# Weights asked for earlier, token columns made later, and two blocks' residual steps sharing the attention: one change to a two-layer fp32 trunk

## The chip, the cores and the metric

The kernel runs on one core of a Trainium2 chip. The metric is the device time of one execution in microseconds (us). The kernel before was timed three times: 2561.57, 2564.88 and 2570.34 us, median 2564.88 us. TensorE is called PE, VectorE DVE, ScalarE ACT, GpSimd POOL, and the queue that issues the DMAs SP.

## The reference

1056 tokens (1024 prompt frames and 32 frames of a running stream) of width 1024 go through two layers in fp32. Each sub-layer normalises its input, and normalises its output before adding it to the residual:

```python
def rms_norm(x, w):
    return x * rsqrt(mean(x * x) + NORM_EPS) * w
# layer 0: gated linear recurrence (HGRN2); layer 1: window attention
x = x + rms_norm(mix, norm_mix_post[layer])
hf = rms_norm(x, norm_ffn_pre[layer])
a, b = split(hf @ w_ffn_in[layer], 2)
x = x + rms_norm((silu(a) * b) @ w_ffn_out[layer], norm_ffn_post[layer])
```

Between the layers, K and V for layer 1 come from one projection of the normalised residual: `k, v = split(rms_norm(x, kv_norm) @ w_kv, 2)`, with a rotation by position on K and on the queries. In layer 1, 16 query heads in 4 groups attend over a window of 128 earlier frames and their own chunk, with a learned sink per head.

## The kernel before

Features lie on the 128 partitions (8 groups, `KT`), tokens along the free axis in three blocks b = 0, 1, 2 of 384, 384 and 288 columns. An fp32 product is three matmuls of split operands: high by high, high by low, low by high. A weight unit is 128x1024 numbers (512 KB): one DMA into `wst` (two buffers), a cast to `wh` on ACT (L102, or L98 where the weight is scaled on the way) and the difference `wl` on DVE (L103, or L99 in four pieces). `wh` and `wl` have four buffers each. `wpair` makes the two units of one column group. The products of a dense stage are L133 (weights stand still, features come out on partitions), L145 (tokens come out on partitions) and L501 (the FFN's output). The accumulators in PSUM (`mm`) have four buffers.

The stages run in this order: the mixer of layer 0; its output projection `outproj` (L133, weights `wao`); the FFN (its input products L133 and L410, its output L501 into `mix`); K, V and Q projections (`kproj`, `vproj1`, `qproj`); the window attention; its `outproj` (weights `wbo`); the second FFN.

The residual's steps are the generator `postnorm`. It sums squares over partitions with a matmul by ones (L180 in `rnorm`, fed by squares on ACT and their running sum `acc` on POOL, L174), takes the inverse root on DVE and ACT (L155 to L163, result `rb`), and then for each of 8 feature groups multiplies (L243) and adds the old residual `xo` (L244), which a DMA brings from DRAM. It splits the result into `xh` (ACT) and `xl` (L210 on DVE), squares it, and sums again for the next norm (a second L180). With `tok=True` a tiny matmul against the identity (L193 in `rcol`) then turns the row `rb` into a token column `rt`; `vproj1` scales V by it.

The caller takes such steps between its own products with `go(generator, n)` and `step(b)`. A scheduler orders each engine's instructions by where they stand in the program and by when they could run; on the chip each engine takes its own list strictly in order, so an instruction that must wait holds all that stand behind it on its engine.

In the FFN's output, block b's products at feature k stand beside the residual's steps of block b-1 by the table `steps`. In the attention, a unit u (0 to 12) is one query group and one 128-token tile: scores `sc` (L1231), a maximum on DVE, exponentials on ACT, a product with the inverse sum (`P`, L1258), transposes `ptp` on PE (L1271), copies `pts`, and the product with V, `pav` (L1289). `plan[b][u]` says which other generators take a step there: `OP[b]` is block b's `outproj` with its residual. `OP[0]` and `OP[1]` use one buffer `mixb` for the projection's output, so that `OP[1]` can't write its output before `OP[0]`'s residual is read.

Of the kernel before, what the change touches and what calls it, by code (L numbers as in the profile page):

```python
# [59 lines left out]
def build(nc, tc, I, O):  # L60
# [45 lines left out]
    def wpair(arr, i, scale=None):  # L106
        return [wunit(arr[2 * i + k], None if scale is None else (scale, 4 * k)) for k in range(2)]
# [107 lines left out]
    def postnorm(b, mix, acc, w2, xold, wnext, spill, yout, done, more=None, full=None, tok=False):  # L215
# [38 lines left out]
        if yout is None:  # L254
# [3 lines left out]
            r = None  # L258
# [19 lines left out]
            done(xs, r, rb)  # L278


    def ffn(L, nx, post1, post, wmix, v1, w2, xold, wnext, spill, yout, res):
# [12 lines left out]
        def fin_half(j, b, half):  # L294
            if j not in wu:
                wu[j] = wpair(I[f"wfi{L}"], j)
# [67 lines left out]
        fin_ev(1, 2, pc, fin_half(1, 2, 1))  # L364
        t123(0)
# [147 lines left out]
        def step(b):  # L513
            if b not in ts:
                c0, W = BL[b]

                def done(*r):
# [4 lines left out]
                                 lambda: mp.tile([128, 384], F32, tag="xo", name="xo", bufs=3), tok=True)  # L522
# [26 lines left out]
        steps = {1: (1, 1, 1, 1, 1, 1, 1, 1), 2: (1, 1, 1, 1, 1, 1, 0, 1)}  # L549
        for b in range(NB):  # L550
            gload(3, b)
        for b in range(NB):
# [4 lines left out]
            def first(k):  # L557
                if k % 2 == 0:
                    un[0] = wfo(2, k // 2)
# [5 lines left out]
            for k in range(KT):  # L565
                if k not in pss:
                    first(k)
                fmul(pss[k], 3, b, wfo(3, k), 0, False, True)
# [51 lines left out]
    mbt = [None] * NB  # L620
    os = [None] * NB
    nx = [None] * NB

    def outproj(b, arr, pre, w2, xold, wnext, spill):
# [3 lines left out]
        mix = mbt[b] = mbs[b].tile([128, KT, 384], F32, tag="mixb", name="mixb", bufs=1)  # L628
# [24 lines left out]
    with tc.tile_pool(name="hp", bufs=1) as hp, \  # L653
# [45 lines left out]
        def vproj(p, b):  # L699
            units = wpair(I["wi"], p)  # L700
            W = BL[b][1]
            vt = vts[p, b] = hp.tile([128, 3, 256], F32, tag="vt", name="vt", bufs=2)
            for jl in range(3):
                rows = min(128, W - jl * 128)
                ps = mmps()
                mm_tm(ps, rows, units, xs[b][0], xs[b][1], jl * 128)
                yield
                nc.scalar.activation(vt[:rows, jl, :], ps[:rows, :256], AF.Copy, scale=rts[b][:rows, jl:jl + 1])  # L708

        v0 = vproj(0, 0)  # L710

        def gproj(p, b):
            units = wpair(I["wg"], p)
# [20 lines left out]
        def stage_a(c, h, b):  # L734
            W = BL[b][1]
            Wp = 384 if W == 384 else 320
            units = first_units if h == b == 0 else wpair(I["wfq"], h)
# [13 lines left out]
            if h == b == 0:  # L751
                go(xl0)
                go(v0)
                go(xl0)
                go(v0)
# [241 lines left out]
        def op0(b):  # L997
            return outproj(b, I["wao"], "a_out", "mix_post0", xin, "ffn_pre0", xs0d)
# [72 lines left out]
    late_pool = [ap, ap, None]  # L1071
# [31 lines left out]

    def kproj(b, units):
# [8 lines left out]
        kb = kbs[b] = late_pool[b].tile([128, 4, 128 + W], F32, name=f"kb{b}")  # L1113
        for du in range(2):
            rs = slice(du * 64, du * 64 + 64)
            if b > 0:
                nc.sync.dma_start(kb[rs, :, 0:128], kds[b - 1].rearrange("g hf r t -> (hf r) g t")[:, :, 256:384])
            nc.sync.dma_start(kb[rs, :, 128:128 + W], kd.rearrange("g hf r t -> (hf r) g t"))
        if b == 2:
# [3 lines left out]
    def vproj1(b, units):  # L1123
# [32 lines left out]
    uk = wpair(I["wk"], 0, scale="kv")  # L1156
# [10 lines left out]
    run(gk)  # L1167
    go(f0)
    uv = wpair(I["wv"], 0, scale="kv")
# [10 lines left out]
    late_pool[2] = ap2  # L1180
    os = [None] * NB
    nx = [None] * NB
    with tc.tile_pool(name="aps", bufs=1, space=PSUM, reuse_waits="tile") as aps:
# [17 lines left out]
        def qload():  # L1201
            b, g = order.pop(0)
            W = BL[b][1]
            qt = ap2.tile([128, 2, W], F32, tag="qt", name="qt", bufs=4)
# [262 lines left out]
```

## Time and profile before

| | |
|---|---|
| median of three runs | 2564.88 us (2561.57 to 2570.34) |
| the profiled execution | 2563.79 us |
| its span, first to last instruction | 2562.0 us |
| mean granted TensorE clock | 0.984 of full |
| PE busy | 2475.2 us, 97% |
| DVE busy | 1714.7 us, 67% |
| ACT busy | 1102.5 us, 43% |
| POOL busy | 451.9 us, 18% |

Times in the views count from the first instruction. A busy PE is not a PE at its full pace: matmuls overlap, and at the lower of its two clocks a matmul that keeps PE busy takes longer. So a stretch is read by three numbers together: busy time, number of matmuls, and granted clock. In a line of waits, "<-" names what the engine waited for.

### The profile page before, as it was taken

The numbers are of one execution on the slowest core, as the hardware profiler recorded it, in microseconds if no ns is written. First come the engines' busy times: TensorE is split into PE (matmuls) and PEld (weight loads), VectorE is DVE, ScalarE is ACT, GpSimd is POOL, SyncE is SP. The second block draws the span as 40 slices with busy tenths as digits, with TensorE's granted clock in tenths as the row PEclk, the third lists the DMA queues.
The fourth block names the chain that finished last, engine by engine and source line by source line (L and its number), as shares of the span: only waits on it lengthen the run. The fifth ranks groups of instructions, "written<-read, shape, count | busy, mean of one in ns | idle before, by whom it ended". The sixth has DMA issues, their size and how long they took to land.

```text
span 2562.0 us, 44049 instructions
## 1 busy us (share of the span) xinstructions
PE 2475.2 (97%) x17124; PEld 2375.9 (93%) x17124; DVE 1714.7 (67%) x3510; ACT 1102.5 (43%) x2395; POOL 451.9 (18%) x644
## 2 busy tenths in 40 slices
PE   7999998999999999999998999989999999999997
PEld 6999998998999999999997997758899999999997
DVE  8888789887776666642467647777876666652456
ACT  6555556665533333341344324556533333342332
POOL 5543444331200000000133311111300000000021
PEclk9999999999999999999999999989999999999998
DMA  5233333443422222251455542223422222252454
GB/s 176 85 104 99 123 121 121 133 133 105 144 77 82 82 79 75 75 174 63 158 164 159 175 132 78 66 71 103 153 87 77 75 75 76 77 176 76 150 174 145
DMA packets 124153, 287.98 MB, mean 112 GB/s; under 512 B 13432, under 2 KB 68632, under 8 KB 123944
## 3 DMA queue, kind: packets, MB, share of 16 engines
q1 hardware_dynamic: 123944, 285.17, 34.9%
q8 instruction: 134, 2.20, 0.3%
q14 instruction: 75, 0.61, 0.1%
HBM read 237.25 MB, written 48.07 MB: 111 GB/s over the span
## 4 chain that ended last, share of the span: by engine, by line
PE 73%; DVE 13%; DMA 5%; ACT 4%; issue 3%; POOL 1%; SPq 0%; POOLq 0%; DVEq 0%; ACTq 0%
PE mm L133 25%; PE mm L501 16%; PE mm L410 14%; PE c L410 6%; PE mm L145 5%; DVE wl L103 2%; PE sc L1231 1%; ACT wh L102 1%; PE pav L1289 1%; PE ptp L1271 1%; DMA xl<-g 1%; DMA wst<-in_wfq 1%; DVE mixb L244 1%; DMA wst<-in_wfo 1%; DVE xl L210 1%
## 5 line engine op out<-in xcount | busy, mean ns | idle before, releaser
L133 PE MATMUL mm<-xh,wh 128*128 128x384 f32 (+1 forms) x1968 | 633.1, 322 | 10.5 <-ACT xh L212 7.5
L133 PE MATMUL mm<-xh,wl 128*128 128x384 f32 (+1 forms) x1968 | 624.7, 317 | 5.3 <-DVE wl L99 3.5
L133 PE MATMUL mm<-xl,wh 128*128 128x384 f32 (+1 forms) x1968 | 625.7, 318 | 2.1 <-DVE xl L213 1.7
L174 POOL TENSOR_TENSOR acc<-acc,tmp 128x384 f32<-128x384 f32 (+1 forms) x168 | 207.4, 1239 | 1710.4 <-ACT tmp L173 1707.7
L103 DVE TENSOR_TENSOR wl<-wst,wh 128x1024 fp32r<-128x1024 f32 (+1 forms) x301 | 373.1, 1244 | 154.5 <-ACT wh L102 153.5
L102 ACT CAST wh<-wst 128x1024 fp32r<-128x1024 f32 (+1 forms) x301 | 313.4, 1046 | 351.1 <-PE mm L501 209.1
L133 PEld LDWEIGHTS mm<-xh,wh 128*128 128x128 f32 x1968 | 373.0, 190 | 18.3 <-ACT xh L212 7.7
L133 PEld LDWEIGHTS mm<-xh,wl 128*128 128x128 f32 x1968 | 373.1, 190 | 14.1 <-issue 5.8
L133 PEld LDWEIGHTS mm<-xl,wh 128*128 128x128 f32 x1968 | 372.8, 189 | 11.5 <-DVE xl L213 5.1
L501 PE MATMUL mm<-xh,wl 128*128 128x384 f32 (+1 forms) x768 | 247.0, 322 | 3.2 <-DVE wl L103 3.2
L501 PE MATMUL mm<-xh,wh 128*128 128x384 f32 (+1 forms) x768 | 247.0, 322 | 0.0
L501 PE MATMUL mm<-xl,wh 128*128 128x384 f32 (+1 forms) x768 | 246.8, 321 | 0.0
L145 PE MATMUL mm<-wh,xh 128*128 128x256 f32 (+1 forms) x648 | 186.7, 288 | 0.8 <-ACT vt L708 0.8
L145 PE MATMUL mm<-wh,xl 128*128 128x256 f32 (+1 forms) x648 | 183.4, 283 | 0.0
L145 PE MATMUL mm<-wl,xh 128*128 128x256 f32 (+1 forms) x648 | 182.9, 282 | 0.0
L394 ACT CAST sh<-sr 128x512 fp32r<-128x512 f32 x144 | 89.5, 622 | 174.0 <-PE mm L410 146.7
L501 PEld LDWEIGHTS mm<-xh,wl 128*128 128x128 f32 x768 | 144.6, 188 | 3.9 <-DVE wl L103 3.9
L501 PEld LDWEIGHTS mm<-xh,wh 128*128 128x128 f32 x768 | 144.5, 188 | 0.2 <-ACT wh L102 0.2
L501 PEld LDWEIGHTS mm<-xl,wh 128*128 128x128 f32 x768 | 144.4, 188 | 0.0
L145 PEld LDWEIGHTS mm<-wh,xh 128*128 128x128 f32 (+1 forms) x648 | 118.1, 182 | 3.5 <-ACT vt L708 0.8
L145 PEld LDWEIGHTS mm<-wh,xl 128*128 128x128 f32 (+1 forms) x648 | 118.2, 182 | 0.7
L145 PEld LDWEIGHTS mm<-wl,xh 128*128 128x128 f32 (+1 forms) x648 | 118.3, 183 | 0.5
(283 smaller groups left out, 5148.1 us busy)
## 6 DMA issues: line engine op xcount, KB each, us to landing
wst<-in_wfo SPq DMA_DIRECT2D x92, 512.0 KB
wst<-in_wfi SPq DMA_DIRECT2D x88, 512.0 KB
wst<-in_wfq SPq DMA_DIRECT2D x47, 512.0 KB
g<-u SPq DMA_DIRECT2D x72, 192.0 KB
wst<-in_wi SPq DMA_DIRECT2D x24, 512.0 KB
wst<-in_wg SPq DMA_DIRECT2D x24, 512.0 KB
wst<-in_wao SPq DMA_DIRECT2D x24, 512.0 KB
xl<-g SPq DMA_DIRECT2D x32, 384.0 KB
```

Source lines behind the costliest of these rows:

```text
L102: nc.scalar.copy(wh[:, s], st[:, s])
L103: nc.vector.tensor_tensor(wl[:, s], st[:, s], wh[:, s].bitcast(F32), sub)
L133: last_mm[0] = nc.tensor.matmul(ps[:, :W], w, x, start=i == 0, stop=i == n - 1)
L145: last_mm[0] = nc.tensor.matmul(ps[:rows, :256], x, w, start=i == 0, stop=i == n - 1)
L174: nc.gpsimd.tensor_tensor(acc[:, :W], acc[:, :W], q[:, :W], add)
L210: nc.vector.tensor_tensor(xl[:, k, :], src, xh[:, k, :].bitcast(F32), sub)
L244: nc.vector.tensor_tensor(m, m, xos[k][:, :W], add)
L394: nc.scalar.copy(h, r)
L410: last_mm[0] = nc.tensor.matmul(ps[:, :384], a, c, start=start and k == i == 0, stop=k == 3 and i == 2, skip_group_check=True)
L501: last_mm[0] = nc.tensor.matmul(ps[:, :W], a, c[:, q, :], start=start and q == i == 0, stop=stop and q == f - 1 and i == 2, skip_group_che ...
L1231: nc.tensor.matmul(pss[pr][:rows, pi, off:off + n], qts[b, g][rsl, pi, qs], kt_[rsl, g, k0:k0 + n], start=pi == 0 and off == lo, stop=samp ...
L1271: nc.tensor.transpose(ptp[:n, hh * rows:hh * rows + rows], P[:rows, hh, off:off + n], ident[:rows, :rows])
```

## The change

1. `wpair` takes a name, and `wahead` makes a pair early and keeps it in `held`, where the next `wpair` finds it. `outproj` asks for the next pair while the current one is used (in layer 0 and layer 1), and in its last round for the FFN's first pair. In the FFN's output, `units()` keeps up to three units asked for, ahead of the residual's steps; the table `steps` starts with (0, 2) in place of (1, 1), and g is loaded block by block. `wv` is asked for behind `wk`, and `wq` before V.
2. `rcol` leaves `postnorm` and is called in `vproj1` behind the first third of V's product.
3. In the attention, K of block 2 is loaded by `kload(2)` at the start of block 1, in a buffer shared with block 0; the query buffers go from four to three; `mixb` becomes one buffer for each of blocks 0 and 1; and `OP[1]`'s projection runs at units 0 to 9 of block 2 beside `OP[0]`'s residual, where before it began at unit 4.
4. In the mixer's start two pieces of `vproj` are taken before the scaling that needs the token column. In the first FFN's input, units 2 and 3 are asked for before `t123`.

```diff
+    def wahead(name, i, scale=None):
+        held[name, i] = wpair(name, i, scale)
...
-            r = None
             rb = cp.tile([128, W], F32, tag=f"rb{b}", name=f"rb{b}")
             rnorm(nacc, rb, W)
             yield
-            if tok:
-                r = cp.tile([128, 3], F32, tag=f"rt{b}", name=f"rt{b}")
-                rcol(rb, W, r)
...
-        steps = {1: (1, 1, 1, 1, 1, 1, 1, 1), 2: (1, 1, 1, 1, 1, 1, 0, 1)}
+        steps = {1: (0, 2, 1, 1, 1, 1, 1, 1), 2: (0, 2, 1, 1, 1, 1, 0, 1)}
...
+        def units():
+            while seq and len(ready) < 3:
+                ready.append(wfo(*seq.pop(0)))
+            if not seq and len(ready) == 1 and yout is None:
+                wahead("wk", 0, scale="kv")
+            return ready.pop(0)
...
             if k % 2 == 0:
                 units = wpair(arr, k // 2, scale=pre)
+                if ahead and k < KT - 2:
+                    wahead(arr, k // 2 + 1, scale=pre)
+                elif ahead:
+                    wahead(*ahead)
...
             mm_tm(ps, rows, units, xh, xl, jl * 128)
+            if jl == 0:
+                rts[b] = cp.tile([128, 3], F32, tag=f"rt{b}", name=f"rt{b}")
+                rcol(rbs[b], W, rts[b])
...
-        plan[2] = {u: [(p, 1)] for u in (0, 1, 2, 3, 5, 6, 8, 9)}
-        for u in range(4, 12):
-            plan[2].setdefault(u, []).append((o, 1))
+        for u in (0, 1, 2, 3, 5, 6, 8, 9):
+            plan[2][u] = [(o, 1)]
+        for u, n in ((0, 1), (1, 1), (3, 1), (5, 1), (7, 2), (8, 1), (9, 1)):
+            plan[2].setdefault(u, []).append((p, n))
+        plan[2][11], plan[2][12] = [(o, 2)], [(o, 1)]
```

The lists of three engines show what moved. Line numbers of the changed kernel are higher: L193 became L201, L180 L188, L133 L141, L145 L153, L243 and L244 L251 and L252, L1271 L1312, L1289 L1330, L1231 L1272.

PE, the token column of block 1, before: it stands inside the rotated K product of block 0 (`mm` from `xh_15451`), and `rb_16277` is the inverse root of block 1.

```order
L133 MATMUL mm<-xl_15452,wh 128x384
L133 MATMUL mm<-xh_15451,wl 128x384
L193 MATMUL mm<-ident,rb_16277 128x1 x3
L133 MATMUL mm<-xh_15451,wh 128x384
L133 MATMUL mm<-xl_15452,wh 128x384
```

The same column after, where `xh_15969` is block 1's input to V:

```order
L153 MATMUL mm<-wh,xh_15969 128x256
L153 MATMUL mm<-wh,xl_15970 128x256
L153 MATMUL mm<-wl,xh_15969 128x256
L201 MATMUL mm<-ident,rb_16295 128x1 x3
L153 MATMUL mm<-wh,xh_15969 128x256
```

The column moved out of block 0's K product into block 1's own V product, 169 rows further on in the list of 14,815.

DVE, the FFN's output of layer 0 at block 2, where the inverse root of block 1's residual ends (`rb_15848` before) and its first multiplies begin; before:

```order
L160 SCALAR_TENSOR_TENSOR rb_15848<-tmp,rb_15848 128x384
L103 TENSOR_TENSOR wl<-wst,wh 128x1024
L162 SCALAR_TENSOR_TENSOR tmp<-tmp,nv 128x384
L163 SCALAR_TENSOR_TENSOR rb_15848<-tmp,rb_15848 128x384
L243 SCALAR_TENSOR_TENSOR mix<-mix,pv,rb_15848 128x384 x2
L244 TENSOR_TENSOR mix<-mix,xo 128x384
```

and after:

```order
L103 TENSOR_TENSOR wl<-wst,wh 128x1024
L170 SCALAR_TENSOR_TENSOR tmp<-tmp,nv 128x384
L171 SCALAR_TENSOR_TENSOR rb_15901<-tmp,rb_15901 128x384
L103 TENSOR_TENSOR wl<-wst,wh 128x1024
L251 SCALAR_TENSOR_TENSOR mix<-mix,pv,rb_15901 128x384 x2
L252 TENSOR_TENSOR mix<-mix,xo 128x384 x2
```

One more weight difference stands right ahead of the first multiply.

PE, the attention of block 2 about unit 2, the transposes of one unit and the scores of the next; before:

```order
L1231 MATMUL sc<-kc,qt 32x128
L1231 MATMUL sc<-kb_17051,qt 32x32
L1271 MATMUL ptp<-ident,P 128x128 x8
L1289 MATMUL pav<-pts,vt 64x256 x2
L1231 MATMUL sc<-kb_17051,qt 128x256
L1289 MATMUL pav<-pts,vt 64x256 x2
L1231 MATMUL sc<-kb_17051,qt 128x256 x3
L1241 LDWEIGHTS mk
```

and after, where L141 is the dense product of `OP[1]`'s projection:

```order
L141 MATMUL mm<-xh_18407,wl 128x384
L141 MATMUL mm<-xh_18407,wh 128x384
L1312 MATMUL ptp<-ident,P 128x128 x8
L141 MATMUL mm<-xl_18408,wh 128x384
L141 MATMUL mm<-xh_18407,wl 128x384
L1330 MATMUL pav<-pts,vt 64x256 x2
L141 MATMUL mm<-xh_18407,wh 128x384
L1272 MATMUL sc<-kb,qt 128x256
L1330 MATMUL pav<-pts,vt 64x256 x2
L1272 MATMUL sc<-kb,qt 128x256 x3
L1282 LDWEIGHTS mk
```

Dense matmuls now stand before the transposes and between the small products, where there were none.

## Rows read from the trace of the kernel before

**Rows 1.** The page: engines' busy time, and the chain that ended last.

```profile
PE 2475.2 (97%) x17124; PEld 2375.9 (93%) x17124; DVE 1714.7 (67%) x3510; ACT 1102.5 (43%) x2395; POOL 451.9 (18%) x644
...
PE 73%; DVE 13%; DMA 5%; ACT 4%; issue 3%; POOL 1%; SPq 0%; POOLq 0%; DVEq 0%; ACTq 0%
```

**Rows 2.** Waits of PE: us in total, times, longest.

```profile
PE mm L180 <- POOL acc L174: 9.7, 4, 3.4
PE mm L193 <- DVE rb L163: 8.1, 3, 5.1
...
PE mm L501 <- DVE wl L103: 6.3, 4, 3.1
PE ptp L1271 <- DVE P L1258: 5.9, 6, 2.1
```

**Rows 3.** Windows: length, busy us (instructions) by engine, clock, DMA share, GB/s.

```profile
640.00:648.00 8.00, 5.55 (x27) 4.13 (x27) 8.00 (x11) 4.27 (x10) 4.27 (x5) 0.89 0.58 190
648.00:656.00 8.00, 8.00 (x48) 7.87 (x47) 2.86 (x4) 3.89 (x7) 3.86 (x4) 0.90 0.83 271
```

**Rows 4.** Windows about the K and V passage, same columns.

```profile
1400.00:1408.00 8.00, 2.92 (x15) 2.28 (x13) 6.12 (x13) 4.68 (x12) 1.59 (x2) 0.75 0.21 70
1408.00:1416.00 8.00, 8.00 (x30) 7.89 (x31) 2.15 (x5) 0.08 (x1) 1.14 (x2) 0.61 0.37 131
...
1416.00:1424.00 8.00, 8.00 (x48) 8.00 (x47) 6.95 (x16) 3.55 (x9) 2.20 (x2) 1.00 0.11 33
...
1456.00:1464.00 8.00, 7.70 (x39) 7.67 (x40) 4.33 (x10) 0.00 (x0) 4.26 (x5) 0.79 0.43 119
```

**Rows 5.** PE in order of time, FFN output of block 1 and after: start, us, [wait].

```profile
1339.03 1.63 PE L180 MATMUL mm<-acc,ones 128*128 128x384 f32 x2 [3.41 <-POOL acc L174]
...
1373.01 0.40 PE L501 MATMUL mm<-xh,wl 128*128 128x288 f32 x1 [1.36 <-DVE wl L103]
...
1379.17 0.40 PE L501 MATMUL mm<-xh,wl 128*128 128x288 f32 x1 [1.10 <-DVE wl L103]
...
1385.72 0.40 PE L501 MATMUL mm<-gh,wl 128*128 128x288 f32 x1 [3.09 <-DVE wl L103]
...
1406.99 1.44 PE L193 MATMUL mm<-ident,rb 128*128 128x1 f32 x6 [5.08 <-DVE rb L163]
```

**Rows 6.** DVE in order of time, FFN output of block 2.

```profile
1371.74 1.21 DVE L103 TENSOR_TENSOR wl<-wst,wh 128x1024 fp32r<-128x1024 f32 x1
...
1375.32 2.66 DVE L244 TENSOR_TENSOR mix<-mix,xo 128x384 f32<-128x384 f32 x2
```

**Rows 7.** Windows of the attention of block 2 and what follows, columns of rows 3.

```profile
1689.00:1722.00 33.00, 25.82 (x129) 15.93 (x130) 26.16 (x58) 15.88 (x56) 7.70 (x7) 0.64 0.29 96
1722.00:1786.00 64.00, 63.24 (x435) 50.59 (x434) 48.27 (x102) 38.76 (x122) 10.80 (x7) 1.00 0.29 91
1786.00:1818.00 32.00, 27.43 (x190) 25.97 (x188) 26.14 (x29) 18.39 (x36) 16.14 (x13) 1.00 0.59 185
```

**Rows 8.** PE in order of time, attention of block 2.

```profile
1698.48 1.94 PE L1271 MATMUL ptp<-ident,P 128*128 128x128 f32 x8 [1.96 <-DVE P L1258]
...
1706.22 1.94 PE L1271 MATMUL ptp<-ident,P 128*128 128x128 f32 x8 [2.13 <-DVE P L1258]
...
1722.10 1.03 PE L1271 MATMUL ptp<-ident,P 128*128 128x128 f32 x8
```

**Rows 9.** DVE in order of time, there and behind it.

```profile
1706.40 0.54 DVE L244 TENSOR_TENSOR mixb<-mixb,xo 128x384 f32<-128x384 f32 x1
...
1710.71 1.34 DVE L244 TENSOR_TENSOR mixb<-mixb,xo 128x384 f32<-128x384 f32 x1
...
1797.44 1.14 DVE L243 SCALAR_TENSOR_TENSOR mixb<-mixb,pv,rb 128x384 f32<-128x384 f32 x2
```

**Rows 10.** PE in order of time, output projection of block 2, layer 1.

```profile
1804.82 0.40 PE L133 MATMUL mm<-xh,wl 128*128 128x288 f32 x1 [0.90 <-DVE wl L103]
...
1818.45 0.91 PE L180 MATMUL mm<-acc,ones 128*128 128x384 f32 x2 [3.21 <-POOL acc L174]
```

More of the change, by code (lines that the diff above doesn't have):

```diff
@@ L104, in wunit, with wpair @@
         return (wh, wl, st) if raw else (wh, wl)
-    def wpair(arr, i, scale=None):
-        return [wunit(arr[2 * i + k], None if scale is None else (scale, 4 * k)) for k in range(2)]
+    held = {}
+    def wpair(name, i, scale=None):
+        if (name, i) in held:
+            return held.pop((name, i))
+        return [wunit(I[name][2 * i + k], None if scale is None else (scale, 4 * k)) for k in range(2)]
+    def wahead(name, i, scale=None):
+        held[name, i] = wpair(name, i, scale)
     first_units = [wunit(I["wfq"][0], pieces=2)]
@@ L213, in put_x, with postnorm @@
             nc.vector.scalar_tensor_tensor(xl[:, k, :], src, pcol(wname, k), xh[:, k, :].bitcast(F32), mult, sub)
-    def postnorm(b, mix, acc, w2, xold, wnext, spill, yout, done, more=None, full=None, tok=False):
+    def postnorm(b, mix, acc, w2, xold, wnext, spill, yout, done, more=None, full=None):
         W = BL[b][1]
@@ L364, in ffn @@
         fin_ev(1, 2, pc, fin_half(1, 2, 1))
+        for j in (2, 3):
+            wu[j] = wpair(f"wfi{L}", j)
         t123(0)
@@ L546, in ffn @@
                     nc.vector.tensor_tensor(dst(k, b), dst(k, b), ps[:, :BL[b][1]], add)
[L549 removed]
+        steps = {1: (0, 2, 1, 1, 1, 1, 1, 1), 2: (0, 2, 1, 1, 1, 1, 0, 1)}
+        gload(3, 0)
+        seq = []
         for b in range(NB):
[L551 removed]
+            for k in range(0, KT, 2):
+                seq += [(2, k // 2), (3, k), (3, k + 1)]
+        seq[:6] = [(2, 0), (2, 1)] + [(3, k) for k in range(4)]
+        ready = []
+        def units():
[4 more added lines that the diff above has]
+            return ready.pop(0)
         for b in range(NB):
@@ L558, in first @@
                 if k % 2 == 0:
-                    un[0] = wfo(2, k // 2)
+                    un[0] = units()
                 pss[k] = mmps()
@@ L567, in ffn @@
                     first(k)
-                fmul(pss[k], 3, b, wfo(3, k), 0, False, True)
+                fmul(pss[k], 3, b, units(), 0, False, True)
+                if k == 1 and b + 1 < NB:
+                    gload(3, b + 1)
                 d = dst(k, b)
@@ L697, in build, with vproj @@
         state = [None] * 8
-        def vproj(p, b):
-            units = wpair(I["wi"], p)
+        def vproj(p, b, ahead=0):
+            units = wpair("wi", p)
             W = BL[b][1]
             vt = vts[p, b] = hp.tile([128, 3, 256], F32, tag="vt", name="vt", bufs=2)
+            pss = []
             for jl in range(3):
@@ L706, in vproj @@
                 mm_tm(ps, rows, units, xs[b][0], xs[b][1], jl * 128)
+                pss.append((jl, rows, ps))
                 yield
-                nc.scalar.activation(vt[:rows, jl, :], ps[:rows, :256], AF.Copy, scale=rts[b][:rows, jl:jl + 1])
-        v0 = vproj(0, 0)
+                if jl >= ahead:
+                    for (i, r, ps) in pss:
+                        nc.scalar.activation(vt[:r, i, :], ps[:r, :256], AF.Copy, scale=rts[b][:r, i:i + 1])
+                    pss.clear()
+        v0 = vproj(0, 0, 1)
         def gproj(p, b):
-            units = wpair(I["wg"], p)
+            units = wpair("wg", p)
             W = BL[b][1]
@@ L1102, in rope, with kload @@
         res.append(a)
+    def kload(b):
+        W = BL[b][1]
+        kb = kbs[b] = ap.tile([128, 4, 512], F32, tag="kb", name="kb", bufs=2)
+        for du in range(2):
+            rs = slice(du * 64, du * 64 + 64)
+            if b > 0:
+                nc.sync.dma_start(kb[rs, :, 0:128], kds[b - 1].rearrange("g hf r t -> (hf r) g t")[:, :, 256:384])
+            nc.sync.dma_start(kb[rs, :, 128:128 + W], kds[b].rearrange("g hf r t -> (hf r) g t"))
     def kproj(b, units):
@@ L1112, in kproj @@
             nc.sync.dma_start(kd[:, hf], a[:, hf, :W])
[L1113 to L1119, printed above, removed]
+        if b < 2:
+            kload(b)
+        else:
             nc.sync.dma_start(O["kp"], a[:, :, 128:256])
```

44 lines of the change are left out of this document (23 added, 21 removed).

## The prediction

> **What bounds the kernel now.** The page comes first: PE is busy for 2475.2 of 2562.0 us, and of the chain that ended last 73% is PE and 13% DVE [rows 1]. So there are no stages to shorten, only holes to fill: about 87 us in which PE does nothing, and what it loses where its clock falls behind a hole. The list of PE's waits names the holes: 9.7 us for POOL's running sum in front of the sums L180, 8.1 us in three L193 for the inverse root, 6.3 us in four L501 for weight differences, 5.9 us in six transposes for `P` [rows 2]. Each is a wait for DVE or for what follows DVE, so in each the question is whether DVE was late because of the order of its work, or because it had too much of it. The windows answer that. Where DVE is busy for all of the window, a new order can only choose who waits. Where it has room, the order was the cause.
>
> The windows also give the price of a hole beyond its length. In 1408 to 1416 PE is busy for the whole 8 us, at a mean granted clock of 0.61 (between its levels of 1.2 and 2.4 GHz), and gets through 30 instructions. In 1416 to 1424, at 1.00, it gets through 48 [rows 4]. The 30 were worth 8 x 30/48 = 5.0 us, so 3.0 us went to the clock. Just ahead of the fall stands the wait of 5.08 us at 1406.99 [rows 5].
>
> **The sum, part by part.** It is made against the profiled execution, 2563.79 us, 1.1 us below the median of 2564.88.
>
> A. *Output projection, layer 0, block 2: weights a pair ahead.* PE idles 8 - 5.55 = 2.45 us in 640 to 648, while DVE is busy for 8.00 of 8. A clock of 0.89 and 0.90 in that window and the next is a fifth of each at the lower level, 3.3 us, half of it lost: 1.7 us [rows 3]. So 4.2 us can go at most. Several differences now stand ahead of residual steps, but the last ones do not. With DVE full I take 2.5, and keep 0 to 4.2.
>
> B. *FFN output, block 1: the table starts (0, 2).* The sum L180 waited 3.41 us for POOL [rows 5]. The squares that feed it come from ACT behind casts that wait for a weight's DMA. Weights asked for earlier should free them. But the residual now begins one product later, and the second L180 stays where it was. I take +1, from -4 (begun later, it ends later) to +3.4.
>
> C. *Token columns.* All three L193 waits go, 8.1 us [rows 2]. Behind the largest the clock cost 3.0 us in 1408 to 1416, and 0.5 us in the window before (a clock of 0.75 is 4 us at the lower level, of which the last 1.0 was work). In 1456 to 1464 PE got through 39 in place of 48, a loss of 1.5 us [rows 4]. Together 13.1. What is late next is known: the column's copy to SBUF now stands on DVE behind residual steps of block 2, and the scaling of V on ACT waits for it, holding up to three of the four PSUM accumulators. The nearest row is the wait it replaces, 5.08 us. Since two thirds of V's product run in the meantime, I charge 1 us and take 12, from 8 to 13.1.
>
> D. *FFN output, block 2: three units ahead.* The waits for `wl` are 1.36, 1.10 and 3.09 us, 5.55 in sum [rows 5]. One difference more stands ahead of the residual's multiplies. It removes one lateness, but not the cause: between two differences lie up to seven DVE operations, two of which took 2.66 us at 1375.32 [rows 6], where one alone takes 0.54 [rows 9]. I take half, 2.8, from 0 to 5.6.
>
> E. *Attention of block 2.* This is the largest hole. From 1689 to 1722 PE is busy for 25.82 of 33 us, idle for 7.2, at a clock of 0.64; in the 64 us behind it PE is busy for 63.24 at 1.00 [rows 7]. The difference is what the list shows: no dense product in the first units, 24 in each later one. A clock of 0.64 means 0.72 x 33 = 24 us at the lower level. Eight transposes take 1.94 us there and 1.03 at the upper [rows 8]. If the some 17 us of work in those 24 shrank like that, 8 us would come back; the score and V products need not shrink as much, and I take 6. So 13.2 us are to be had. The dense products that fill the hole are taken out of units 4, 7, 10 and 11, where the next block's projection, or what the scheduler holds over, stands between the small products. What it costs is room on DVE. In the two windows it worked 26.16 + 48.27 = 74.4 us. Six operations of `OP[1]`'s inverse root, at about 0.54 like one L244 [rows 9], and its first residual pair, 1.14 for two multiplies [rows 9] and 1.08 for two adds, come to about 5.5 more. 80 us of DVE in 97 - 13 = 84 us leaves little slack in a chain where PE waits for `P` in every unit. I take 10, from 2 to 13.2.
>
> At 1710.71 one add of 0.54 us took 1.34 [rows 9], in a window where POOL was at work too. The Trainium skill ("SBUF — State Buffer", section "SBUF: two separate sides") says that DVE and POOL share a port pair under an exclusive lock, held for a whole instruction, against a DVE operation with two SBUF inputs. The row agrees. By that rule each POOL sum moved into this fuller stretch can cost DVE up to 0.8 us, 1.6 us for the two that come with the joined pair. That would make the 10 about 8.4.
>
> F. *Output projection, layer 1, block 2.* Waits of 0.90 us for `wl` and 3.21 us for POOL's sum at L180 [rows 10], 4.1 in sum, where DVE was busy for 26.14 of 32 us [rows 7]. The inverse root and first pair are gone from here, about 5.5 us of DVE, and weights come earlier. I take 3.5, from 0 to 4.1.
>
> G. *The rest:* V before the first column, units 2 and 3 before `t123`, block by block `g`, weights of V and Q, the second FFN's output. The engines' lists of the mixer are the same, so the start moves nothing; at the other places PE did not wait. SP now takes K of block 2 ahead of some `wbo` units, and one query buffer is gone; a pair of weights asked for ahead covers a few us. 0, from -3 to +2.
>
> Sum: 2.5 + 1 + 12 + 2.8 + 10 + 3.5 + 0 = 31.8. 2563.8 - 31.8 = 2532.
>
> **The rivals.**
> *DVE is the limit (0.16).* At A, D and F it is saturated, and the waits only change owner: 0. B loses 4. In E the chain through `P` gives back 4 in place of 10. C stays, 12. Sum 12: 2552. For it: 8.00 of 8 in rows 3, and 80 of 84 us above. Against it: PE and DVE both have room over the whole of 1689 to 1818 (100.6 us of DVE in 129).
> *Slower: softmax behind the joined steps (0.05).* In the attention of block 2, the residual's steps and the weights' differences now stand between a unit's scores and its `P` from unit 0 on. If every unit's transposes wait as those at 1698 and 1706, 1.96 and 2.13 us [rows 8], 13 units give 27 us; and if the clock falls there for the 97 us as it did for 33, with 6 lost per 33, 18 us more. 45 us against the 21.8 of the other parts: 2563.8 + 23 = 2587. It decides from about 1 us a unit, where with its clock it eats the other parts. Against it: from 1722 on residual steps already stood there, and PE was idle for 0.8 us in 64 [rows 7].
> *The hole only moves (0.07).* Units 10 to 12 have no step of a projection in the plan. If the idle time and low clock reappear there, E is 2: 2540.
> *The columns don't do what they should (0.05).* The copy is late by as much as the largest wait, in two of the three blocks: 10 us and 3 for the clock off C: 2545.
> The forecast has the remaining 0.67.
>
> **How the numbers follow.** The forecast's own range is 2520 to 2545: 2518 is every part at its best, about 2561 every one at its worst, neither of them likely. With the rivals at 2552, 2540 and 2545 inside, the range 2515 to 2555 leaves the slower rival and the tails out. About 0.3%, 7.7 us, is what a measurement can tell from no change. Faster by more holds in the forecast and three rivals, but for their tails: 0.89. The same: 0.06, from parts at their worst. Slower: 0.05.
>
> **What would show it.** C is right if no wait for the inverse root above 1 us is left between 1340 and 1460, and the clock there stays at 1.00 behind block 1's product. E is right if the window from the end of block 1's attention on has PE above 95% busy at 1.00, and wrong if `ptp` waits for `P` in most units. A, D and F are right if waits for `wl` sum to less than half of before. B shows in the wait of L180 for POOL. The prediction is wrong as a whole if PE's waits for DVE and POOL in the sum fall by less than 10 us, or new waits for DMA (K, queries, `xo`) appear.

## The result, and the profile after

The changed kernel took 2546.08 us (median of four runs, 2543.42 to 2551.49), the kernel before 2566.32 us beside it: the ratio is 0.9924, with a 95% interval of 0.9904 to 0.9943. That is 20.2 us faster, where 31.8 were forecast; 2546 lies inside the range of 2515 to 2555. In the profiled executions the span went from 2562.0 to 2546.8 us. In one run below (the column first and the first FFN undone) one of six executions took 3835.55 us at a mean granted clock of 0.58, and the ratio given there is of the other five. The page of the changed kernel, busy time by engine, answers [rows 1]:

```profile
span 2546.8 us, 44040 instructions
...
PE 2469.6 (97%) x17124; PEld 2373.7 (93%) x17124; DVE 1722.0 (68%) x3510; ACT 1101.2 (43%) x2395; POOL 457.5 (18%) x644
```

The counts of these five rows are the same as before: the change moves work and removes none. PE's idle time fell from 86.8 to 77.2 us (span less busy). The other 5.6 us of the span are busy time; the mean granted clock went from 0.984 to 0.988.

PE's waits in the changed kernel (us in total, times, longest), against [rows 2]:

```profile
PE mm L188 <- POOL acc L182: 10.1, 3, 7.1
...
PE mm L507 <- DVE wl L103: 4.9, 3, 3.0
...
PE ptp L1312 <- DVE P L1299: 3.0, 5, 1.2
```

The 8.1 us for the inverse root are gone from the list, the transposes' wait is halved, and the wait for weight differences in L507 (L501 before) is down from 6.3 to 4.9. The wait for POOL has not shrunk: the four waits with 3.4 as the longest became three, the longest of 7.1.

A change that touches many places is best read by stages. The marks in this table are starts of PE's instructions, the first or last of a line; the lengths are in us. "Mixer" ends with the last transpose of the recurrence (L992 before), "projection 0" with the first L410 of layer 0, "FFN output 0" runs from the first to the last L501 there, "K, V, Q" ends with the first score (L1231), "attention" with the first L410 of layer 1 (so it has the second output projection and the FFN's first products in it), and "FFN output 1" is as in layer 0. What is left out, 377.1 us in each FFN and some 17.6 at the end, is equal in all.

| kernel | mixer | projection 0 | FFN output 0 | K, V, Q | attention | FFN output 1 | span |
|---|---|---|---|---|---|---|---|
| before | 618.5 | 128.3 | 272.7 | 127.3 | 386.4 | 257.0 | 2562.0 |
| changed | 620.4 | 126.3 | 272.5 | 122.8 | 377.7 | 255.4 | 2546.8 |
| changed, second profile | 619.8 | 125.8 | 271.0 | 123.3 | 372.8 | 255.9 | 2540.4 |
| columns alone | 619.6 | 128.0 | 266.7 | 121.6 | 387.6 | 257.6 | 2553.2 |
| attention alone | 618.0 | 126.5 | 273.1 | 127.1 | 377.4 | 258.6 | 2552.3 |
| weights alone | 617.5 | 127.1 | 276.1 | 130.6 | 386.8 | 255.2 | 2565.0 |
| old table, block 1 | 620.4 | 128.5 | 269.2 | 122.4 | 372.9 | 255.6 | 2540.9 |
| same, second profile | 620.7 | 126.2 | 271.2 | 122.4 | 375.6 | 254.6 | 2542.3 |
| column first | 623.8 | 128.0 | 272.6 | 121.0 | 374.2 | 255.2 | 2546.5 |
| old table, block 1, and column first | 621.6 | 128.6 | 268.9 | 121.2 | 377.5 | 255.7 | 2545.4 |
| first FFN's output undone | 619.8 | 126.4 | 269.3 | 122.1 | 374.3 | 255.8 | 2539.3 |
| same, and column first | 618.0 | 126.4 | 269.8 | 119.5 | 377.8 | 255.4 | 2538.6 |
| fill later | 621.0 | 127.6 | 271.8 | 122.3 | 373.3 | 255.3 | 2543.1 |

The attention gave 8.7 us in one profile and 13.6 in the other, K, V and Q some 4, the second FFN's output 1.1 to 1.6. The first FFN's output gave nothing or 1.7, though two of the forecast's terms and part of a third lie there. The rows also show how far a stage moves with no change in its own code: 372.8 to 377.8 us for the attention with the new plan, 125.8 to 128.6 for projection 0 with weights ahead, 617.5 to 623.8 for the mixer.

The hole in the attention is filled. The windows of the changed kernel over the same stretch (from the first units of block 2 on; columns as in [rows 3]), to be held against [rows 7]:

```profile
1684.00:1717.00 33.00, 32.07 (x219) 24.68 (x217) 32.10 (x63) 21.45 (x64) 10.97 (x8) 1.00 0.49 154
1717.00:1781.00 64.00, 61.21 (x388) 47.22 (x388) 48.02 (x108) 36.44 (x120) 8.52 (x6) 0.90 0.23 74
1781.00:1813.00 32.00, 29.85 (x187) 29.03 (x186) 24.43 (x26) 19.58 (x37) 17.59 (x14) 0.94 0.65 214
```

In the first 33 us PE is now busy for 32.07 at a clock of 1.00, where it was 25.82 at 0.64. DVE is busy for 32.10 of the same 33: both engines are full. In the next 64 us the clock is 0.90 where it was 1.00, so in this profile part of the loss has moved on; in the second profile it is 0.97 there.

The passages of the changed kernel, PE in order of time, answering [rows 5]:

```profile
1341.96 1.65 PE L188 MATMUL mm<-acc,ones 128*128 128x384 f32 x2 [7.11 <-POOL acc L182]
...
1386.62 0.40 PE L507 MATMUL mm<-xh,wl 128*128 128x288 f32 x1 [3.04 <-DVE wl L103]
...
1393.31 0.40 PE L507 MATMUL mm<-xh,wl 128*128 128x288 f32 x1 [1.64 <-DVE wl L103]
...
1471.10 0.58 PE L153 MATMUL mm<-wh,xh 128*128 128x256 f32 x1 [1.89 <-DVE tmp L1130]
...
1479.15 0.41 PE L141 MATMUL mm<-xh,wh 128*128 128x384 f32 x1 [0.83 <-DVE rt L205]
```

The sum in front of the second norm, L188, waits 3.7 us longer than before. Two new waits stand behind the columns (L153 and L141), and the longest of the old ones (5.08 us at 1406.99) has no successor.

### The profile page after: what moved, and what is told of

Read it like the earlier page. It is cut to its first block, busy times and chain, and to the rows that moved or that the text cites. A ratio compares the mean times of both kernels' runs of the same rounds, so it can differ in the third digit from the quotient of the medians.

```text
span 2546.8 us, 44040 instructions
## 1 busy us (share of the span) xinstructions
PE 2469.6 (97%) x17124; PEld 2373.7 (93%) x17124; DVE 1722.0 (68%) x3510; ACT 1101.2 (43%) x2395; POOL 457.5 (18%) x644
## 4 chain that ended last, share of the span: by engine, by line
PE 74%; DVE 12%; DMA 5%; ACT 4%; issue 3%; POOL 1%; SPq 0%; POOLq 0%; DVEq 0%; ACTq 0%
PE mm L141 23%; PE mm L507 18%; PE mm L416 14%; PE c L416 6%; PE mm L153 5%; DVE wl L103 2%; PE sc L1272 2%; PE pav L1330 1%; ACT wh L102 1%; PE ptp L1312 1%; DVE wl L99 1%; DMA wst<-in_wfq 1%; DMA xl<-g 1%; DVE mixb L252 1%; DMA xo<-in_x 1%
## 5 line engine op out<-in xcount | busy, mean ns | idle before, releaser
L141 PE MATMUL mm<-xh,wh 128*128 128x384 f32 (+1 forms) x1968 | 632.9, 322 | 11.1 <-ACT xh L220 7.5
L141 PE MATMUL mm<-xh,wl 128*128 128x384 f32 (+1 forms) x1968 | 624.3, 317 | 5.5 <-DVE wl L99 3.0
L141 PE MATMUL mm<-xl,wh 128*128 128x384 f32 (+1 forms) x1968 | 627.1, 319 | 2.0 <-DVE xl L221 1.3
L103 DVE TENSOR_TENSOR wl<-wst,wh 128x1024 fp32r<-128x1024 f32 (+1 forms) x301 | 379.3, 1264 | 145.0 <-ACT wh L102 144.4
L141 PEld LDWEIGHTS mm<-xh,wh 128*128 128x128 f32 x1968 | 372.8, 190 | 20.9 <-ACT xh L220 7.5
L141 PEld LDWEIGHTS mm<-xh,wl 128*128 128x128 f32 x1968 | 373.0, 190 | 13.8 <-issue 5.6
L141 PEld LDWEIGHTS mm<-xl,wh 128*128 128x128 f32 x1968 | 372.6, 189 | 13.2 <-issue 4.7
L507 PE MATMUL mm<-xh,wl 128*128 128x384 f32 (+1 forms) x768 | 247.1, 322 | 4.7 <-DVE wl L103 4.7
L507 PE MATMUL mm<-xh,wh 128*128 128x384 f32 (+1 forms) x768 | 247.1, 322 | 0.0
L507 PE MATMUL mm<-xl,wh 128*128 128x384 f32 (+1 forms) x768 | 247.0, 322 | 0.0
L153 PE MATMUL mm<-wh,xh 128*128 128x256 f32 (+1 forms) x648 | 189.1, 292 | 3.2 <-DVE tmp L1130 2.2
L153 PE MATMUL mm<-wh,xl 128*128 128x256 f32 (+1 forms) x648 | 185.0, 285 | 0.0
L153 PE MATMUL mm<-wl,xh 128*128 128x256 f32 (+1 forms) x648 | 184.6, 285 | 0.0
L507 PEld LDWEIGHTS mm<-xh,wl 128*128 128x128 f32 x768 | 144.5, 188 | 5.2 <-DVE wl L103 5.2
L507 PEld LDWEIGHTS mm<-xl,wh 128*128 128x128 f32 x768 | 144.4, 188 | 0.0
L507 PEld LDWEIGHTS mm<-xh,wh 128*128 128x128 f32 x768 | 144.4, 188 | 0.0
L153 PEld LDWEIGHTS mm<-wh,xh 128*128 128x128 f32 (+1 forms) x648 | 119.9, 185 | 6.3 <-DVE tmp L1130 2.4
L153 PEld LDWEIGHTS mm<-wh,xl 128*128 128x128 f32 (+1 forms) x648 | 120.0, 185 | 0.7
L153 PEld LDWEIGHTS mm<-wl,xh 128*128 128x128 f32 (+1 forms) x648 | 119.9, 185 | 0.5
```

The costliest lines, as they stand in the source:

```text
L103: nc.vector.tensor_tensor(wl[:, s], st[:, s], wh[:, s].bitcast(F32), sub)
L141: last_mm[0] = nc.tensor.matmul(ps[:, :W], w, x, start=i == 0, stop=i == n - 1)
L153: last_mm[0] = nc.tensor.matmul(ps[:rows, :256], x, w, start=i == 0, stop=i == n - 1)
L507: last_mm[0] = nc.tensor.matmul(ps[:, :W], a, c[:, q, :], start=start and q == i == 0, stop=stop and q == f - 1 and i == 2, skip_group_che ...
```

## The experiments

**Three parts, each alone on the kernel before.** First the columns: `rcol` in `vproj1`, and no `tok=True`.

```diff
             mm_tm(ps, rows, units, xh, xl, jl * 128)
+            if jl == 0:
+                rts[b] = cp.tile([128, 3], F32, tag=f"rt{b}", name=f"rt{b}")
+                rcol(rbs[b], W, rts[b])
             yield
```

> The kernel before with only the token columns moved behind the first third of V's product. Theory: it removes the waits of 1.2, 5.1 and 1.9 us for the inverse root and the clock behind them (some 13 us) and brings new waits of 3 to 6 us: 7 to 10 us faster than before. Rival: the gain of that stage in the changed kernel came from weights asked for early, and the columns alone give less than 4 us.

Measured: 2556.11 against 2563.55 us, ratio 0.9967 (0.9951 to 0.9983), 7.4 us. By stages the FFN's output became 6.0 us shorter and K, V, Q 5.7, together 11.7; the other stages gave back 2.9 (span -8.8). The time lies in the theory's range, with an interval of 4.4 to 12.6 us; PE's new waits in K, V, Q come to 4.4 us (waits of 0.3 us and more). One thing doesn't fit: of the three column waits before, only the first, of 1.21 us, stands in the FFN's output.

```profile
1349.03 0.83 PE L193 MATMUL mm<-ident,rb 128*128 128x1 f32 x6 [1.21 <-DVE rb L163]
...
1456.30 0.76 PE L193 MATMUL mm<-ident,rb 128*128 128x1 f32 x6 [1.85 <-DVE rb L163]
```

So the 6.0 us of that stage are more than this wait explains, and the two runs below that have the same code in this stage (the first FFN undone) took 269.3 and 269.8 us in it, 3.4 and 2.9 less than before.

Then the attention: two `mixb` buffers, the new plan, `kload(2)`, three query buffers, three steps behind the loop in place of six.

```diff
-        plan[2] = {u: [(p, 1)] for u in (0, 1, 2, 3, 5, 6, 8, 9)}
-        for u in range(4, 12):
-            plan[2].setdefault(u, []).append((o, 1))
+        for u in (0, 1, 2, 3, 5, 6, 8, 9):
+            plan[2][u] = [(o, 1)]
+        for u, n in ((0, 1), (1, 1), (3, 1), (5, 1), (7, 2), (8, 1), (9, 1)):
+            plan[2].setdefault(u, []).append((p, n))
+        plan[2][11], plan[2][12] = [(o, 2)], [(o, 1)]
```

> The kernel before with only the attention's part of the change (two buffers for the projection's output, the new plan, K of block 2 loaded later, three query buffers), without weights a pair ahead. Theory: the hole in the first units of block 2 is filled and block 1's first residual steps leave the output projection: 8 to 13 us faster than before, from the first score to the second FFN 374 to 379 us in place of 386.5. Rival: the gain there comes from weights a pair ahead; then it is under 4 us, with waits for weight differences above 2 us in the projection.

Measured: 2554.25 against 2565.04 us, ratio 0.9962 (0.9950 to 0.9975), 10.8 us; the stage took 377.4. Its window shows the same as in the whole change:

```profile
1684.00:1717.00 33.00, 31.87 (x224) 24.51 (x226) 31.61 (x65) 22.52 (x70) 8.98 (x8) 1.00 0.46 142
```

PE is busy for 31.87 of 33 at full clock without any weight asked for ahead. The longest wait for a difference in the projection behind it was 2.49 us, so the rival had a true part, but the gain does not hang on it.

Then the weights: everything of points 1 and 4 of the change with `rcol` in `postnorm` and the attention as before.

```diff
+    def wahead(name, i, scale=None):
+        held[name, i] = wpair(name, i, scale)
...
+        steps = {1: (0, 2, 1, 1, 1, 1, 1, 1), 2: (0, 2, 1, 1, 1, 1, 0, 1)}
```

> The kernel before with only the weights asked for earlier (in the output projections, in the FFN's outputs with the new table, about K, V and Q, in the first FFN's input and at the start), with columns and attention as before. Theory: by the stages this is what costs time in the first FFN's output and gains about 2 us each in the two output projections and the second FFN's output: within 4 us of the kernel before, either way, with L180 waiting for POOL over 6 us at about 1340. Rival: the weights carry part of the gain of the passage and the attention: 6 us faster or more.

Measured: 2569.91 against 2565.04 us, ratio 1.0021 (1.0010 to 1.0032): 4.9 us slower, clear of its interval, a little more than the theory's 4. PE in order of time shows where:

```profile
1339.98 1.65 PE L188 MATMUL mm<-acc,ones 128*128 128x384 f32 x2 [7.11 <-POOL acc L182]
...
1410.63 1.01 PE L201 MATMUL mm<-ident,rb 128*128 128x1 f32 x4 [5.74 <-DVE rb L171]
...
1460.91 0.76 PE L201 MATMUL mm<-ident,rb 128*128 128x1 f32 x6 [3.04 <-DVE rb L171]
```

The wait for POOL is the 7.11 us of the whole change. The columns, still in their old place, wait 5.74 and 3.04 us where they waited 5.08 and 1.85. So the part that was to hide waits made three of them longer. The three spans differ from that of before by -8.8, -9.7 and +3.0, in sum -15.5; the whole change has -15.2 in one profile and -21.6 in the other. By spans the parts add up, within the spread of one kernel's profiles. By the medians of the timed runs they come to 13.3 us (7.4 + 10.8 - 4.9), against 20.2 for the whole, each with an interval of some 3 to 4 us either way. A part of that gap has a reason in the stages: the weights make K, V, Q 3.3 us longer while the columns stand in their old place, and 1.2 to 1.7 once these are moved (122.8 and 123.3 against 121.6). The rest is not settled.

**What made L188 late.** In the changed kernel, the end of block 1 (POOL, ACT and DVE in order of time):

```profile
1337.41 5.45 POOL L182 TENSOR_TENSOR acc<-acc,tmp 128x384 f32<-128x384 f32 x4 [2.88 <-ACT tmp L181]
```

```profile
1335.45 0.51 ACT L217 CAST xh<-mix 128x384 fp32r<-128x384 f32 x1 [4.47 <-DVE mix L252]
1335.87 1.04 ACT L102 CAST wh<-wst 128x1024 fp32r<-128x1024 f32 x1
1336.81 1.35 ACT L181 ACTIVATE tmp<-mix 128x384 f32<-128x384 f32 x3
```

```profile
1331.63 2.03 DVE L103 TENSOR_TENSOR wl<-wst,wh 128x1024 fp32r<-128x1024 f32 x1
1333.58 1.36 DVE L218 TENSOR_TENSOR xl<-mix,xh 128x384 fp32r<-128x384 f32 x1
1334.87 0.55 DVE L252 TENSOR_TENSOR mix<-mix,xo 128x384 f32<-128x384 f32 x1
```

POOL still has four sums to do at 1337.41, 5.45 us of work, while PE has been idle since 1334.85. It waited for squares; ACT had three of them in its list behind the cast L217 of the residual's last group and one cast of a weight, and L217 waited 4.47 us for L252, the last add of block 0's residual, on a DVE without a pause. To try this, the old table was put back for block 1 alone:

```diff
-        steps = {1: (0, 2, 1, 1, 1, 1, 1, 1), 2: (0, 2, 1, 1, 1, 1, 0, 1)}
+        steps = {1: (1, 1, 1, 1, 1, 1, 1, 1), 2: (0, 2, 1, 1, 1, 1, 0, 1)}
```

> The changed kernel with the old table (1, 1, 1, ...) for block 1 of the FFN's output, all else kept. Theory: the sum L188 waits 7.1 us for POOL at 1342 (3.4 before) because the residual of block 0 starts one product later and its last steps fall on the last squares; with the old table the wait is 4 us or less, and with the clock the kernel gains 4 to 6 us on the changed one. Rival: the units asked for ahead, whose differences stand on DVE ahead of the block's last adds, make it late; then the wait stays at 6 us or more and the time within 1 us.

Measured: 2542.89 us, ratio 0.9908 (0.9882 to 0.9934). The wait and what holds the squares now, PE and ACT:

```profile
1341.81 1.65 PE L188 MATMUL mm<-acc,ones 128*128 128x384 f32 x2 [4.48 <-POOL acc L182]
```

```profile
1335.67 1.05 ACT L102 CAST wh<-wst 128x1024 fp32r<-128x1024 f32 x1 [2.58 <-DMA wst<-in_wfo]
1336.63 1.34 ACT L181 ACTIVATE tmp<-mix 128x384 f32<-128x384 f32 x3
```

The table is worth 2.6 us of the wait, a little less than the theory asked for. With the residual out of the way, the squares stand behind a cast that waits for its weight's DMA. That was so in the kernel before, and the wait there was shorter:

```profile
1333.79 1.05 ACT L102 CAST wh<-wst 128x1024 fp32r<-128x1024 f32 x1 [1.32 <-DMA wst<-in_wfo]
```

So at this place asking for the units earlier did not make the cast earlier. The gain on the changed kernel, 3.2 us, was of the size of the spread, so both were timed again on one chip (below).

Then all of that part was undone in the first FFN alone: no units ahead (nor the first of `wk`), the old table for both blocks, g at once.

```diff
+        early = yout is not None
-            while seq and len(ready) < 3:
+            while seq and len(ready) < (3 if early else 1):
```

> The changed kernel with the first FFN's output as before: weight units not asked for ahead, g loaded at once, the old table; the second FFN keeps the change. Theory: this part of the change costs time. From the first product of the FFN's output to the last, the kernel before took 272.7 us with the three columns, the changed one 272.5 without them, and the kernel before with the columns alone moved 266.8; so undone here it should take 266 to 268, and the kernel gain 4 to 7 us on the changed one. Rival: the table alone was the fault (the old table for block 1 gave 269.3), and units asked for ahead help block 2: then the stage takes 270 or more and the kernel is no faster than with the table alone, 2543 us.

Measured: 2545.42 us, ratio 0.9927 (0.9915 to 0.9940). The stage took 269.3 us, between theory and rival, and the kernel is no faster than the changed one: the theory falls as far as units ahead go. L188 waits 3.54 us there, but block 2's waits for differences are 1.67, 1.11 and 3.10 us, 5.9 in sum, as before the change. With units ahead and the old table for block 1 they are 4.48 and 0.67 + 3.04. So units ahead, together with block 2's table and g block by block, cost about 0.9 us at L188 and gain 2.2 in block 2, and the new table for block 1 costs 2.6. The three were not tried one by one.

**The new waits behind the columns.** The column was taken ahead of V's first product:

```diff
+            if jl == 0:
+                rts[b] = cp.tile([128, 3], F32, tag=f"rt{b}", name=f"rt{b}")
+                rcol(rbs[b], W, rts[b])
             ps = mmps()
             mm_tm(ps, rows, units, xh, xl, jl * 128)
```

> The changed kernel with the token column taken ahead of V's first product in place of behind it. Theory: the new waits of PE at 1471 (1.9 us, for the rotation's temporaries on DVE), 1479 (0.8) and about 1420 come from accumulators held because the column's copy is late; with the column one product (4 us) earlier they fall to under 1 us in sum, a gain of 3 to 4.5 us with the clock. Rival: they come from the rotated K and Q products waiting on a DVE that is busy with scaled weight differences; then the waits stay, and the column itself waits for the inverse root again (up to 1.9 us): no gain, or 2 us lost.

Measured: 2546.02 us, ratio 0.9916 (0.9884 to 0.9949): no gain that can be seen in the time. K, V, Q took 121.0 us, 1.8 less than in the changed kernel, about half of what the theory said. The first wait is

```profile
1475.96 0.38 PE L153 MATMUL mm<-wh,xh 128*128 128x256 f32 x1 [0.62 <-DVE tmp L1130]
```

in place of 1.89; with two others, of 0.86 and 0.56 us, the waits behind the columns come to 2.0 us in place of 3.1 (waits of 0.3 us and more), where the theory asked for under 1. DVE's list in the changed kernel shows why it was not the copy alone:

```profile
1470.23 0.46 DVE L1129 TENSOR_TENSOR ra<-mm,cosr 128x288 f32<-128x288 f32 x1 [3.49 <-DMA qd<-ra]
1470.60 0.45 DVE L1130 TENSOR_TENSOR tmp<-mm,sinr 128x288 f32<-128x288 f32 x1
```

L1129 waits 3.49 us for the DMA that empties a buffer of the rotated K and Q, and L1130, for which PE waits, stands behind it. In the kernel before, DVE's waits for this transfer (`qd<-ra`) came to 2.6 us in two, in the changed kernel to 8.9 us in two. With the column first the same wait is 3.23 us. Neither theory had named this transfer. Other buffers for it were not tried, so that it holds PE up is read from the list, not shown by a run.

The column first and the first FFN undone were then run together:

> The one before, and the token column taken ahead of V's first product. Theory: the two gains add: 4 to 7 us for the FFN's output, and the 1 to 2 us that the stage from K to the attention gained in the run with the column first (121.1 us against 122.8): 2537 to 2541 us. Rival: the waits of that stage grow back when the FFN's output ends earlier, and it is the same as the one before within 1 us.

Measured: 2545.07 us, ratio 0.9914 (0.9899 to 0.9929), equal to the one before; K, V, Q took 119.5 us. The theory's 2537 to 2541 was not reached.

**The end of the attention.** The dense products were kept for later units:

```diff
-        for u in (0, 1, 2, 3, 5, 6, 8, 9):
+        for u in (0, 1, 2, 4, 5, 7, 9, 10):
             plan[2][u] = [(o, 1)]
```

> The changed kernel with the projection of block 1 at units 0, 1, 2, 4, 5, 7, 9, 10 of the attention of block 2 in place of 0, 1, 2, 3, 5, 6, 8, 9. Theory: the two stretches at half clock at 1754 to 1761 and 1774.5 to 1781 are there because the last units have no dense product; moved to later units they go, gaining 3 to 5 us. Rival: the last units wait for DVE and ACT, full with block 1's inverse root, and dense products moved there only take the place of block 2's; the time stays within 1 us, or the sum L188 waits for POOL and up to 3 us are lost.

Measured: 2544.30 us, ratio 0.9913 (0.9886 to 0.9939); the stage took 373.3 us. That looks like the 3 to 5 us of the theory, but with the changed kernel's plan the run with the old table took 372.9, the one with the column first 374.2 and the changed kernel's second profile 372.8. So the plan made no difference that can be told, and the theory's reason falls.

**The changed kernel once more, and two candidates, on one chip.** Here the changed kernel is repeated:

> The changed kernel once more, beside the two below. Theory: about 2546 us, with the stages of the first profile within 1 us where the clock falls behind the same waits, and up to 5 us off in the attention and the mixer where it falls a different number of times. Rival: the stages repeat within 1 us everywhere, and the 3 to 5 us between the attention stage of the changed kernel (377.7 us) and of runs with the same code there (372.9, 374.2) come from what precedes it.

Measured: 2546.55 us, ratio 0.9915 (0.9899 to 0.9931). Its waits repeat to 0.02 us at L188 and L507 (7.11 and 3.04); shorter ones do not, 1.64 us at L507 is gone and 0.83 at L141 is 0.30. The attention took 372.8 us in place of 377.7. The lists of PE, DVE, ACT and POOL are in the same order in both. The stretch between two waits that both have, 1.01 us of L1272 and 1.20 us of L1312, first in the changed kernel's first profile, then in its second:

```profile
1752.36:1773.91 21.55, 20.32 (x124) 15.48 (x125) 16.34 (x36) 12.05 (x39) 1.00 (x1) 0.84 0.38 121
```

```profile
1750.31:1769.00 18.69, 17.39 (x124) 13.53 (x125) 16.09 (x36) 12.01 (x39) 0.99 (x1) 1.00 0.45 140
```

The same 124 matmuls take 2.9 us less at a clock of 1.00 than at 0.84, and PE idles for 1.2 and 1.3 us. So the theory holds for the attention: a wait of about 1 us is followed by the lower clock in one execution and not in another, and 2.9 of the 4.9 us lie in this stretch. It does not hold everywhere: the first FFN's output took 271.0 us in place of 272.5. The chip alone is not what decides: two more runs on this chip (below), with the same code in the attention, took 375.6 and 377.5 us there. Then the old table for block 1 again, and with the column first:

> The changed kernel with the old table for block 1, once more and on the same chip as the changed kernel. Theory: L180's wait for POOL near 1342 is 4.5 us in place of 7.1, and the kernel is 2 to 4 us faster than the changed one. Rival: the 3 us between their medians so far were the spread of either: equal within 1 us.

> The old table for block 1 and the token column ahead of V's first product, both on the changed kernel. Theory: the two gains add, 2 to 4 us and 1 to 2 us: 2540 to 2543 us, the fastest of the three. Rival: the column's gain is lost in the spread, as in the run that had it alone: equal to the one with the table within 1 us.

Measured: 2543.86 us (2540.18 to 2545.10), ratio 0.9902 (0.9886 to 0.9918), and 2543.70 us (2539.31 to 2547.20), ratio 0.9898 (0.9879 to 0.9917). L188 waits 4.50 and 4.59 us. Both medians are under that of the changed kernel, by 2.7 and 2.9 us, within the theory's 2 to 4 for the table, while the second stays just above its 2540 to 2543. The intervals overlap with the changed kernel's, so it is likely but not settled that they are faster than it; over both pairs of runs, eight executions with the old table alone took 2540.2 to 2545.1 us and nine of the changed kernel 2542.1 to 2551.7. The column's gain does not show in the time, though K, V, Q is shorter by 1.8, 2.6 and 1.2 us in the three pairs of profiles. The old table for block 1 is the best version that the runs point to.

## Why the prediction was right, and what in it was not

The direction and the mechanisms of the two large terms (C and E) were right. The range held, but it was 40 us wide. The sum was 12 us too large (31.8 against 20.2), most of it in K, V, Q and in the first FFN's output, and this is where it went.

- A, 2.5 forecast: not shown. The stage gave 2.0 and 2.5 us in the two profiles of the change, -0.3 to 2.1 in the other runs with weights ahead, and 1.8 in the run with the attention alone, which has the old code there (126.5 us). PE's idle time in it did not fall, 4.5 us before and 5.3 in the changed kernel; what rose is the clock, from 0.97 to 1.00, and in the run with the old table it was 0.97 again. The waits of [rows 3] are replaced by one of 2.08 us for `wl` and one of 1.01 us at L188.
- B, +1 forecast: a step that failed. "Weights asked for earlier should free them" did not come true, and nearly the end of the bracket was reached: the wait grew from 3.41 to 7.11 us, -3.7. The old table brings it to 4.48, and there the cast in front of the squares waits 2.58 us for its weight's DMA, where it waited 1.32. The residual begun one product later ends on the block's last squares; DVE had no slack to take that up.
- C, 12 forecast: the mechanism was right, the size not, and the 11.7 by stages of the run with the columns alone is in part luck. By the prediction's rows 1.2 us of it lay in the FFN's output, and the rest, with the clock and less the charge of 1 us, some 11, in K, V, Q. That run gave 6.0 and 5.7, and the same code gave 2.9 and 3.4 in the FFN's output elsewhere. In the whole change K, V, Q gained 4.0 to 4.5. PE's idle time there fell from 6.9 to 4.2 us only (4.7 with the columns alone): "I charge 1 us" was too little, the new waits of 1.89 and 0.83 us are 2.7 alone. The rest is clock, and less of it than the 5.0 us that were counted.
- D, 2.8 forecast: 5.55 us of waits became 3.04 + 1.64 in one profile and 3.04 in the other, and 3.10 + 1.67 + 1.11 without units ahead became 3.04 + 0.67 with them and the old table for block 1. 0.9 to 2.5: right in kind, somewhat short in size. In the length of the stage B's loss took it up.
- E and F, 13.5 together: 8.7 and 13.6 us, 8.6 to 13.5 in the other runs with this plan and weights ahead, and 9.0 with the attention alone (10.8 by its time). The fill did what was said ([rows 7] against the windows above). The whole forecast is reached where the clock holds, and some 5 us less where it falls at the end of the attention. In F the 3.21 us at L180 are gone, but the waits for `wl`, of which the prediction had left out 0.68 and 0.23 us, did not shrink (1.8 us before, 2.2 and 2.7 after). One step of the working for E does not carry over to other cases: it added 6 us of clock to 7.2 us of idle time. With the attention as before, the first stretch ran at a higher clock in the run with the columns alone. The same 110 matmuls, from the wait of L1271 at 1688.95 to that of L180 at 1717.13 before, and there:

```profile
1688.95:1717.13 28.18, 21.00 (x110) 12.89 (x111) 23.33 (x51) 13.26 (x48) 7.70 (x7) 0.65 0.31 104
```

```profile
1678.48:1705.44 26.96, 17.73 (x110) 10.92 (x111) 23.94 (x51) 13.16 (x48) 8.07 (x7) 0.87 0.32 108
```

  PE's busy time fell by 3.3 us, its idle time rose from 7.2 to 9.2, and the stretch is 1.2 us shorter; the whole stage took 387.6 us against 386.4. Where PE waited for DVE in every unit, most of what the clock gave back here went into longer waits. In the change dense products took the place of the waits, and PE was busy at 1.00.
- G, 0 forecast: the second FFN's output gained 1.1 to 1.6 us, in line with all runs (254.6 to 255.9 us with weights ahead, 257.0 to 258.6 without). The mixer was 1.3 to 1.9 us longer, within its spread.

Of the rivals, "DVE is the limit" was right at B, and at A the runs don't tell its 0 from the forecast; E and F did not shrink to 4 and 0. "The hole only moves" was half right in one profile (0.84 at the end of the attention) and not in the other. The columns did what they should, but for the copy: PE waited 0.83 us for an accumulator that it held (1.61 and 1.32 with the columns alone), far from the rival's 10. Softmax did not fall behind: the transposes' waits for `P` fell from 5.9 to 3.0 us.

The signs named ahead: no wait for the inverse root is left between 1340 and 1460, as said for C, and the clock is 1.00 in every 8 us from 1404 to 1468; in the next 8, about the new wait of 1.89 us, it is 0.79. PE is over 95% busy at 1.00 in the first 33 us of E's window (32.07 of 33), and as busy at 0.90 behind it. For A, D and F the waits for `wl` were to fall to less than half, and they did not: from 3.5 to 2.5 us, from 5.6 to 4.9 and from 1.8 to 2.2 (2.6, 3.3 and 2.7 in the second profile). The prediction was to be wrong as a whole if PE's waits for DVE and POOL fell by less than 10 us. They fell from 53.9 us to 44.2 and 42.7, by 9.7 and 11.2, which is just on that line. PE has no new wait for DMA; DVE has, for `qd<-ra`, from 2.6 to 8.9 us, which the prediction had not priced.

That the residual's later start puts L188 back, by 2.6 of the 3.7 us, is shown by the table's runs. That the lower clock in one profile of the attention does not come from the code is shown by two profiles of one kernel; what decides it stays open. So does why the old columns waited longer with weights ahead: that DVE's list has more in front of the inverse root is argued, not tried.

## What to carry to other kernels

Before work is put ahead or put off, ask whether the engines that prepare it have slack: on a DVE that worked without a pause, the residual begun one product later ended on the block's last squares, and those fed PE's next sum. Don't add waits and a low clock in the same stretch while PE still waits for another engine's chain: here 2.1 of the 3.3 us that a faster clock gave back went into longer waits. And a wait that is removed exposes the next latest one, so price that one by name (here, by DVE's list, a DMA that empties a buffer) and not by a lump.

## What the runs showed of the hardware

The longest waits of one kernel repeated to 0.02 us between two profiles (7.11, 3.04), shorter ones to 0.3 (1.89 and 2.18 for L153) or not at all (1.64 for L507). Where the lower clock fell behind such waits did not repeat: the same 124 matmuls, behind the same wait of 1.01 us, took 21.55 us at 0.84 in one profile and 18.69 at 1.00 in the other, with the same idle time to 0.1 us, and a 375 us stage moved by 5 us. A stage's length from one profile is good to a few us for that reason, and a difference of 3 us between two kernels needs the waits themselves, or repeated timing, to be believed.
